# Modulation units as row products with a kept sum on VectorE, from a transposed weight

## The chip, the cores and the metric

One NeuronCore of a Trainium2 chip runs the whole program. The metric is the device time of one execution in microseconds. All tensors are float32; large products are split into a high and a low part in the rounded f32 format (fp32r), so that one product is three matmuls.

## What is computed

One inference step of a small diffusion backbone: two layers over 128 context tokens and 512 latent tokens of width 1024. Each layer is half a feed-forward block, a mixer of three head groups, and another half feed-forward block. Each of the three parts is modulated by vectors that come from a conditioning vector. Cut to what the change touches:

```python
def rmsnorm(x, g):
    y = x * lax.rsqrt(jnp.mean(x * x, axis=-1, keepdims=True) + EPS)
    return y * g

def layer(h, mod, p, lam_init, ctx):
    sh1, sc1, gt1, sh2, sc2, gt2, sh3, sc3, gt3 = jnp.split(mod[:, None, :], 9, axis=-1)
    u = rmsnorm(h, p["g_norm"][0]) * (1.0 + sc1) + sh1
    h = h + 0.5 * gt1 * swiglu(u, p["w_ff_in"][0], p["w_ff_out"][0])
    u = rmsnorm(h, p["g_norm"][1]) * (1.0 + sc2) + sh2
    y, cache = mix(u, p, lam_init, ctx)
    h = h + gt2 * y
    u = rmsnorm(h, p["g_norm"][2]) * (1.0 + sc3) + sh3
    h = h + 0.5 * gt3 * swiglu(u, p["w_ff_in"][1], p["w_ff_out"][1])
    return h, cache

for l in range(2):
    mod_ctx = silu(c_ctx)[None, :] @ w_ada[l] + b_ada[l]     # w_ada[l]: 1024 x 9216
    mod_lat = silu(c) @ w_ada[l] + b_ada[l]
    hp, cache_l = layer(hp, mod_ctx, p, lam_init, None)
    hs, _ = layer(hs, mod_lat, p, lam_init, ctx_l)
```

The two products with `w_ada` are what the change is about: two vectors of 1024 against a matrix of 1024 x 9216 in each layer, 75 MB of weights in all.

## The kernel before

**Layout.** The state h lies transposed in SBUF, features on partitions, tokens along the row (8 tiles of 128 x 640). All tokens, context and latent, go through one stream of products. The program runs, per layer: the first feed-forward half (FFN), the mixer (projection, three attentions, an order of work made by a planner of the kernel's own), the output projection (`wout`), and the second FFN half. A startup phase with an order written out by the planner stands ahead.

**An FFN half** (`ffn`) goes over 22 slices of the hidden width in four groups (6, 6, 5 and 5 slices). The first three slices are plain products in two token halves (`plain0`, `plain1`), the others a Strassen-like form of seven products per slice (`wino`). For each slice the weights are loaded (`load1`, 1 MB, two buffers shared with the other weight loads), and ScalarE and VectorE make the high and low parts. After the slices of a group come four steps `dd` of output products (`load2`, `unit2`), each followed by `update`, in which VectorE adds the gated PSUM result to h. The last group ends in `tail`, which starts the norm of the next part (`stats`, `norm`, `u_steps`): ScalarE squares, POOL and VectorE add them up, TensorE sums over partitions, and VectorE and ScalarE form the modulated input u.

**The modulations** come in 72 units of 256 columns of `w_ada` (`ada_units`), 36 per layer, in the order in which they are needed. The first 8 belong to startup. The other 64 are handed out by `pump`, which stands after slices (`pin`) and after output steps (`pout`); the table `ADA` says where and of which kind, one pair for each of the four FFN halves. A unit loads its 1024 x 256 block in two halves of 512 KB (`ada_raw`, tag `adaw`, two buffers, rows of 1 KB) on the SP queue. There are two kinds:

- "P" (`ada_unit_pe`, 21 of them): TensorE multiplies the blocks by the conditioning columns in strips of 32 columns (`ada_strip`, tile `adp`), ScalarE copies the result (`adrow`), and TensorE folds and turns it (tile `adt`).
- "D" (`ada_unit`, 43 of them): VectorE multiplies each of the eight 128 x 256 blocks by one conditioning value per partition and adds up, for both vectors (16 passes, `adacc`); TensorE transposes the two sums (4 transposes, `adt`), and VectorE reduces them along the row (`adred`).

`ada_finish` then adds the bias and forms the gates and scales (`mod`).

**What sets the order.** Each engine works its instructions in order. Outside the parts that the kernel's planner lays out, the order on each engine is made at build time by the framework, which goes by the order of the program and by when it expects an instruction to be ready: strips and VectorE passes of a unit are mixed into the surrounding slice work, and loads are put on the SP queue ahead of their use as buffers come free. PSUM has four small slots (`ps1`) and two large ones (`ps2`) for all of this; a slice's large slot is free once its SwiGLU steps (`post_steps`) have read it. `wpair`/`split` make the weight parts, `mm` (line 192) is the helper through which most matmuls go.

Of the kernel before, what the change touches and what calls it, by code (L numbers as in the profile page):

```python
# [32 lines left out]

_OUT = {(g, dd): "D" for g in (0, 6, 12, 17) for dd in range(2 if g == 17 else 3)}
ADA = (
    ({0: "P", **dict.fromkeys(range(2, 11), "P"), 14: "D", 16: "D", 19: "D"}, _OUT),
    ({0: "P", **dict.fromkeys((2, 3, 4), "P"), 8: "D", 14: "D", 19: "D"}, _OUT),
    ({**dict.fromkeys((4, 7, 10), "P"), 8: "D", 13: "D", 16: "D", 19: "D"}, _OUT),
    ({0: "P", **dict.fromkeys((2, 3, 4), "P")}, {}),
)  # L40
NP_ = 3
# [140 lines left out]
class Net:  # L182
# [139 lines left out]
    def ada_raw(self, l, s, u):  # L322

        c0 = s * D + u * 256
        for e in range(0, KD, QK):
            raw = self.adp.tile([P, QK, 256], F32, tag="adaw", name="adaw", bufs=2)
            self.nc.sync.dma_start(raw, self.a["w_ada"][l, e * P : (e + QK) * P, c0 : c0 + 256].rearrange("(k p) c -> p k c", p=P))
            for k in range(QK):
                yield e + k, raw[:, k, :]

# [4 lines left out]

    def ada_unit(self, l, s, u):
        nc, a = self.nc, self.a
        pt = self.ps1("adt")
        acc = [self.adp.tile([P, 256], F32, tag="adacc", name="adacc", bufs=2) for v in range(2)]
        for k, raw in self.ada_raw(l, s, u):  # L340
            for v in range(2):
                col = self.cs[:, 8 * v + k : 8 * v + k + 1]
                if k == 0:
                    nc.vector.tensor_scalar(acc[v], raw, col, None, ALU.mult)
                else:
                    nc.vector.scalar_tensor_tensor(acc[v], raw, col, acc[v], ALU.mult, ALU.add)  # L346
        for v in range(2):
            for j in range(2):
                nc.tensor.transpose(pt[:, (2 * v + j) * P : (2 * v + j + 1) * P], acc[v][:, j * P : (j + 1) * P], self.ident)
        red = self.sm.tile([P, 2, 2], F32, tag="adred", name="adred")  # L350
        nc.vector.tensor_reduce(red, pt.rearrange("p (v j c) -> p v j c", v=2, j=2), AX.X, ALU.add)
        self.ada_finish(l, s, u, red)

    def ada_unit_pe(self, l, s, u):

        ps = self.ps1("adp")
# [2148 lines left out]
```

## Time and profile before

| | us |
|---|---|
| median of 3 runs | 2755.49 (2755.48 to 2758.77) |
| profiled execution, its own time | 2755.85 |
| its span, first to last instruction | 2754.1 |
| TensorE matmul busy | 2671.8 |
| VectorE busy | 2147.6 |
| ScalarE busy | 1274.6 |
| mean granted TensorE clock | 0.987 |

The profile is one execution, with each instruction's start and duration. PE is TensorE's matmul row, DVE VectorE, ACT ScalarE, POOL GpSimd, SP the engine that issues the loads. Matmul durations overlap, since they are pipelined: the time that one takes up in the stream is the distance to the start of the next. A line number can be that of a helper; the names of the tiles (out<-in) tell what an instruction is for.

### The profile page before, as it was taken

Reading aid. Unit: us, or ns where it says so; the run is one execution under the profiler, and the core shown is the slowest. Engines: PE = TensorE matmul, PEld = TensorE weight load, DVE = VectorE, ACT = ScalarE, POOL = GpSimd, SP = SyncE. Lnnn points to the kernel's source line nnn. Section 1 sums busy time; section 2 is a strip of 40 time slices with the busy share of each in tenths; the row PEclk is TensorE's granted clock in tenths of the full one; section 3 lists DMA queues with packets and bytes.
Section 4 is the critical chain, followed back from the end, with each engine's and each line's share of the span. In section 5 each row is a group of like instructions: output and inputs, shape, how many; then the busy total and the mean of one; then the engine's idle time right before and its main releaser. Section 6 shows DMA issues by size and latency. Waiting matters only on the chain.

```text
span 2754.1 us, 46045 instructions
## 1 busy us (share of the span) xinstructions
PE 2671.8 (97%) x17549; PEld 2478.5 (90%) x17549; DVE 2147.6 (78%) x4580; ACT 1274.6 (46%) x2929; POOL 310.3 (11%) x506
## 2 busy tenths in 40 slices
PE   7999999999999999999999999999999999999998
PEld 5898999888778899999989999998887798999998
DVE  6687899776886678898987889987768847676765
ACT  5424334466675442433444334345657734343433
POOL 1000000142522100000010000003443220000000
PEclk8999999999999999999999999999999999999999
DMA  7454443322103324344333443433211033322232
GB/s 236 139 154 142 119 123 111 120 95 89 40 3 96 99 82 135 95 129 122 100 93 92 123 138 110 143 120 107 83 50 39 3 115 92 92 71 78 75 87 75
DMA packets 363348, 276.39 MB, mean 100 GB/s; under 512 B 25128, under 2 KB 350840, under 8 KB 363128
## 3 DMA queue, kind: packets, MB, share of 16 engines
q1 hardware_dynamic: 363128, 273.45, 33.2%
q8 instruction: 139, 2.28, 0.4%
q14 instruction: 81, 0.66, 0.1%
HBM read 259.25 MB, written 14.16 MB: 99 GB/s over the span
## 4 chain that ended last, share of the span: by engine, by line
PE 85%; DVE 7%; ACT 4%; POOL 1%; DMA 1%; issue 1%; SPq 0%; POOLq 0%; DVEq 0%; ACTq 0%
PE gu L192 35%; PE w L192 20%; PE zps L192 8%; PE ga L192 5%; PE wo L192 4%; PE tr L1294 3%; PE num L192 2%; PE sc L192 1%; PE y L1963 1%; PE z L192 1%; PE y L192 1%; PE adp L334 1%; DVE mx L1702 1%; DVE adacc L346 1%; DMA adaw<-in_w_ada 1%
## 5 line engine op out<-in xcount | busy, mean ns | idle before, releaser
L192 PE MATMUL gu<-u,wH 128*128 128x320 f32 x3504 | 625.8, 316 | 10.6 <-DVE pm L670 3.7
L192 PE MATMUL w<-hid,wH 128*128 128x384 f32 (+1 forms) x2816 | 621.1, 311 | 2.1 <-ACT wH L212 1.1
L192 PEld LDWEIGHTS gu<-u,wH 128*128 128x128 f32 x3504 | 542.3, 191 | 36.8 <-ACT X L1006 8.0
L192 PE MATMUL gu<-u,wL 128*128 128x320 f32 x3120 | 565.9, 314 | 1.6 <-DVE X L1008 0.6
L192 PEld LDWEIGHTS gu<-u,wL 128*128 128x128 f32 x3120 | 483.3, 189 | 19.9 <-ACT X L1006 6.6
L192 PEld LDWEIGHTS w<-hid,wH 128*128 128x128 f32 x2816 | 471.0, 188 | 7.5 <-ACT hid L694 3.6
L192 PE MATMUL w<-hid,wL 128*128 128x256 f32 (+1 forms) x1408 | 431.7, 310 | 0.9 <-DVE wL L213 0.8
L192 PEld LDWEIGHTS w<-hid,wL 128*128 128x128 f32 x1408 | 263.9, 188 | 2.5 <-DVE wL L213 2.3
L221 ACT CAST wH<-raw 128x512 fp32r<-128x512 f32 x266 | 163.6, 620 | 205.9 <-PE w L192 81.8
L346 DVE SCALAR_TENSOR_TENSOR adacc<-adaw,cs,adacc 128x256 f32<-128x256 f32 x602 | 255.5, 480 | 0.0
L739 POOL TENSOR_TENSOR ssum<-ssum,sq 128x384 f32<-128x384 f32 (+1 forms) x36 | 36.1, 1003 | 1886.3 <-ACT sq L738 1794.1
L192 PE MATMUL zps<-wH,u 128*128 128x512 f32 x704 | 242.0, 404 | 1.8 <-ACT u L888 1.7
L221 ACT CAST wL<-raw 128x512 fp32r<-128x512 f32 x266 | 163.9, 620 | 165.3 <-PE w L192 57.5
L931 DVE SCALAR_TENSOR_TENSOR h<-w,mod,h 128x128 f32<-128x128 f32 (+1 forms) x384 | 155.1, 436 | 105.4 <-PE w L192 104.3
L212 ACT CAST wH<-raw 128x640 fp32r<-128x640 f32 (+2 forms) x148 | 120.5, 816 | 223.7 <-PE w L192 161.9
L222 DVE TENSOR_TENSOR wH<-raw,wH 128x512 fp32r<-128x512 f32 x266 | 182.5, 688 | 42.8 <-ACT wH L221 40.9
L222 DVE TENSOR_TENSOR wL<-raw,wL 128x512 fp32r<-128x512 f32 x266 | 182.5, 688 | 38.0 <-ACT wL L221 36.7
L192 PEld LDWEIGHTS zps<-wH,u 128*128 128x128 f32 x704 | 131.8, 188 | 33.4 <-ACT u L888 5.3
L213 DVE TENSOR_TENSOR wL<-raw,wH 128x640 fp32r<-128x640 f32 (+2 forms) x148 | 137.7, 933 | 28.3 <-PE gu L192 14.6
L694 ACT CAST hid<-th 128x320 fp32r<-128x320 f32 x176 | 80.9, 459 | 148.7 <-DVE th L689 148.2
L192 PE MATMUL zps<-wL,u 128*128 128x512 f32 x352 | 138.0, 392 | 0.0
L1708 ACT ACTIVATE pr<-sc,mx 128x640 f32<-128x640 f32 (+1 forms) x160 | 113.5, 711 | 34.3 <-DVE mx L1702 33.2
(357 smaller groups left out, 4355.3 us busy)
## 6 DMA issues: line engine op xcount, KB each, us to landing
raw<-in_w_ff_in SPq DMA_DIRECT2D x176, 512.0 KB
adaw<-in_w_ada SPq DMA_DIRECT2D x144, 512.0 KB
raw<-in_w_ff_out SPq DMA_DIRECT2D x32, 768.0 KB
raw<-in_w_ff_out SPq DMA_DIRECT2D x32, 640.0 KB
rawi<-in_w_in SPq DMA_DIRECT2D x16, 1024.0 KB
rawo<-in_w_out SPq DMA_DIRECT2D x8, 1024.0 KB
bspill<-z SPq DMA_DIRECT2D x20, 256.0 KB
rawi<-in_w_in SPq DMA_DIRECT2D x8, 512.0 KB
```

The lines of the kernel that those rows point to most:

```text
L192: self.nc.tensor.matmul(out, lhsT, rhs, start=start, stop=stop, skip_group_check=go_on)
L212: nc.scalar.copy(H, raw)
L213: nc.vector.tensor_tensor(L, raw, H.bitcast(F32), ALU.subtract)
L221: nc.scalar.copy(w[:, 0], raw)
L222: nc.vector.tensor_tensor(w[:, 1], raw, w[:, 0].bitcast(F32), ALU.subtract)
L334: self.nc.tensor.matmul(ps[j : j + 32, 0:256], self.cs32[:, k, :], raw, start=k < 4, stop=k >= 4, tile_position=(0, j))
L346: nc.vector.scalar_tensor_tensor(acc[v], raw, col, acc[v], ALU.mult, ALU.add)
L694: nc.scalar.copy(self.hid[q][:, 0, c], st["th", hf])
L739: (nc.gpsimd if d in SSG else nc.vector).tensor_tensor(ssum[:, :w], ssum[:, :w], sq[:, :w], ALU.add)
L931: nc.vector.scalar_tensor_tensor(hh, ps[:, s0:s1], gm[:, v, d : d + 1], hh, ALU.mult, ALU.add)
L1294: nc.tensor.transpose(pt[:, i * P : (i + 1) * P], x, ident)
L1708: nc.scalar.activation(o, view(), AF.Exp, bias=bx["mx"], accum_out=bx["sums"])
```

## The change

All 64 units after startup are made in one way: `w_ada` is laid out transposed by the host, so that a block of 128 output columns is 128 rows of 1024. A unit loads two such blocks (512 KB each, 4 KB per partition), and for each block and each of the two vectors VectorE multiplies the rows by the conditioning vector, which is broadcast to all partitions, and keeps the sum along the row. Nothing of it goes through TensorE, PSUM or ScalarE. The broadcast vectors are made once after startup (`ada_rows`: two loads of 512 KB from one row each, two tanh passes of 1024 columns on ScalarE, two passes on VectorE). The first eight units stay on TensorE and read a copy of their columns in the old layout. The tables say how many units stand at a place: 20 in the first FFN half, 18 in the second and third, and two after each of the first two steps of both output projections (8); the units are used up before the fourth FFN half, whose entries find none left. The pump ahead of the second token half of slices 0 and 1 in `ffn` (`pin.get(0)`) is dropped. The DMA scratch in SBUF, which the framework reserves for descriptors that GpSimd writes, is set to 1 KB per partition.

```diff
-_OUT = {(g, dd): "D" for g in (0, 6, 12, 17) for dd in range(2 if g == 17 else 3)}
+_OUT = {(g, dd): n for g in (0, 6, 12, 17) for dd, n in enumerate((1, 1) if g == 17 else (2, 1, 1))}
 ADA = (
-    ({0: "P", **dict.fromkeys(range(2, 11), "P"), 14: "D", 16: "D", 19: "D"}, _OUT),
-    ({0: "P", **dict.fromkeys((2, 3, 4), "P"), 8: "D", 14: "D", 19: "D"}, _OUT),
-    ({**dict.fromkeys((4, 7, 10), "P"), 8: "D", 13: "D", 16: "D", 19: "D"}, _OUT),
-    ({0: "P", **dict.fromkeys((2, 3, 4), "P")}, {}),
+    (dict.fromkeys((3, 5, 8, 10, 14, 16), 1), _OUT),
+    (dict.fromkeys((4, 8, 14, 19), 1), _OUT),
+    (dict.fromkeys((4, 8, 14, 19), 1), _OUT),
+    (dict.fromkeys((3, 4), 1), {(0, 0): 2}),
 )
+ADO = 2, 2
...
+    def ada_rows(self):
+
+        nc = self.nc
+        self.csr = self.cp.tile([P, 2, D], F32, name="csr")
+        nc.sync.dma_start(self.csr[:, 0], self.a["c"][0].partition_broadcast(P))
+        nc.sync.dma_start(self.csr[:, 1], self.a["c_ctx"].partition_broadcast(P))
+        for v in range(2):
+            th = self.adp.tile([P, D], F32, tag="adaw", name="csth", bufs=2)
+            nc.scalar.activation(th, self.csr[:, v], AF.Tanh, scale=0.5)
+            nc.vector.scalar_tensor_tensor(self.csr[:, v], th, 1.0, self.csr[:, v], ALU.add, ALU.mult)
+
     def ada_unit(self, l, s, u):
-        nc, a = self.nc, self.a
-        pt = self.ps1("adt")
-        acc = [self.adp.tile([P, 256], F32, tag="adacc", name="adacc", bufs=2) for v in range(2)]
-        for k, raw in self.ada_raw(l, s, u):
+
+        nc = self.nc
+        red = self.sm.tile([P, 2, 2], F32, tag="adred", name="adred")
+        for j in range(2):
+            raw = self.adp.tile([P, D], F32, tag="adaw", name="adaw", bufs=2)
+            c0 = s * D + u * 256 + j * P
+            nc.sync.dma_start(raw, self.a["w_ada"][l, c0 : c0 + P])
             for v in range(2):
-                col = self.cs[:, 8 * v + k : 8 * v + k + 1]
-                if k == 0:
-                    nc.vector.tensor_scalar(acc[v], raw, col, None, ALU.mult)
-                else:
-                    nc.vector.scalar_tensor_tensor(acc[v], raw, col, acc[v], ALU.mult, ALU.add)
-        for v in range(2):
-            for j in range(2):
-                nc.tensor.transpose(pt[:, (2 * v + j) * P : (2 * v + j + 1) * P], acc[v][:, j * P : (j + 1) * P], self.ident)
-        red = self.sm.tile([P, 2, 2], F32, tag="adred", name="adred")
-        nc.vector.tensor_reduce(red, pt.rearrange("p (v j c) -> p v j c", v=2, j=2), AX.X, ALU.add)
+                out = self.adp.tile([P, D], F32, tag="adout", name="adout", bufs=1)
+                nc.vector.scalar_tensor_tensor(out, raw, 0.5, self.csr[:, v], ALU.mult, ALU.mult, accum_out=red[:, v, j : j + 1])
         self.ada_finish(l, s, u, red)
-
-    def ada_unit_pe(self, l, s, u):
...
     def startup(self, np_stack):
...
-                    nc.sync.dma_start(raws[i, e], a["w_ada"][l, e * 512 : (e + 1) * 512, c0 : c0 + 256].rearrange("(k p) c -> p k c", p=P))
+                    nc.sync.dma_start(raws[i, e], a["w_ada0"][e * 512 : (e + 1) * 512, c0 : c0 + 256].rearrange("(k p) c -> p k c", p=P))
...
         man.close()
+        self.ada_rows()
...
     def pump(self, kinds):
-        for e in kinds:
+        for e in range(kinds):
             x = next(self.adaq, None)
             if x is not None:
-                (self.ada_unit if e == "D" else self.ada_unit_pe)(*x)
+                self.ada_unit(*x)
...
     def ffn(self, l, j, gs):
...
-                self.pump(pin.get(0, ""))
...
     def wout(self, l):
...
                 for e in range(2):
                     for hf in range(2):
                         unit(2 * dd + e, hf)
+                self.pump(ADO[dd])
...
-    nc = _bacc.Bacc("TRN2", target_bir_lowering=False, num_devices=1)
+    nc = _bacc.Bacc("TRN2", target_bir_lowering=False, num_devices=1, dynamic_dma_scratch_size=1024)
...
+    host["w_ada0"] = np.ascontiguousarray(host["w_ada"][0, :, : 2 * D])
+    host["w_ada"] = np.ascontiguousarray(host["w_ada"].transpose(0, 2, 1))
```

## Rows read from the trace of the kernel before

**Rows 1.** The page's busy line: busy us (share of the span) and instructions by engine.
```profile
PE 2671.8 (97%) x17549; PEld 2478.5 (90%) x17549; DVE 2147.6 (78%) x4580; ACT 1274.6 (46%) x2929; POOL 310.3 (11%) x506
```
**Rows 2.** Stretches: three FFN halves, output projection; columns named in the first line.
```profile
core 0: us, PE busy (x) PEld busy (x) DVE busy (x) ACT busy (x) POOL busy (x), PEclk, DMA share, GB/s
75.00:515.00 440.00, 436.69 (x2951) 414.08 (x2949) 366.74 (x791) 166.05 (x323) 2.49 (x3) 1.00 0.44 131
960.00:1400.00 440.00, 438.78 (x2932) 427.27 (x2925) 382.15 (x814) 173.54 (x333) 6.28 (x6) 0.99 0.38 113
1450.00:1868.00 418.00, 415.18 (x2782) 403.53 (x2783) 366.48 (x790) 163.54 (x316) 3.31 (x4) 1.00 0.41 122
878.00:928.00 50.00, 50.00 (x337) 50.00 (x336) 20.93 (x40) 14.45 (x24) 11.15 (x8) 1.00 0.44 137
```
**Rows 3.** TensorE's timeline, one P unit: start us, us, engine, line, operation, tiles, count.
```profile
205.73 1.63 PE L192 MATMUL gu<-u,wL 128*128 128x320 f32 x10
207.29 1.05 PE L334 MATMUL adp<-adaw,cs 128*32 128x256 f32 x10
208.27 2.03 PE L192 MATMUL gu<-u,wH 128*128 128x320 f32 x12
210.23 0.63 PE L334 MATMUL adp<-adaw,cs 128*32 128x256 f32 x6
210.79 1.29 PE L192 MATMUL gu<-u,wL 128*128 128x320 f32 x7
211.92 0.50 PE L192 MATMUL adt<-fold,adrow 128*128 128x2 f32 x4
212.28 0.98 PE L192 MATMUL gu<-u,wL 128*128 128x320 f32 x5
```
**Rows 4.** TensorE's timeline, the transposes of one D unit.
```profile
162.82 0.28 PE L192 MATMUL w<-hid,wL 128*128 128x256 f32 x1
162.94 0.60 PE L349 MATMUL adt<-ident,adacc 128*128 128x128 f32 x4
163.30 0.59 PE L192 MATMUL w<-hid,wH 128*128 128x384 f32 x2
```
**Rows 5.** TensorE's timeline, start of the second FFN half of layer 0.
```profile
933.52 0.75 PE L192 MATMUL gu<-u,wH 128*128 128x320 f32 x4
...
938.13 0.62 PE L192 MATMUL gu<-u,wL 128*128 128x320 f32 x1
...
953.76 0.31 PE L192 MATMUL gu<-u,wL 128*128 128x320 f32 x1
...
960.72 0.90 PE L192 MATMUL gu<-u,wH 128*128 128x320 f32 x2
```
**Rows 6.** VectorE's timeline in the same stretch.
```profile
936.74 1.22 DVE L213 TENSOR_TENSOR wL<-raw,wH 128x1024 fp32r<-128x1024 f32 x1
...
959.30 0.48 DVE L689 TENSOR_TENSOR th<-th,gu 128x320 f32<-128x320 f32 x1
```
**Rows 7.** TensorE's timeline, start of layer 1's first FFN half; brackets: idle before, releaser.
```profile
1443.73 0.90 PE L192 MATMUL gu<-u,wH 128*128 128x320 f32 x2 [3.70 <-DVE pm L670]
```
**Rows 8.** Groups by line and shape: count | busy us, mean ns | idle before, releasers.
```profile
L1589 DVE TENSOR_TENSOR wL<-rawi,wH 128x1024 fp32r<-128x1024 f32 x32 | 39.4, 1246 | 9.7 <-ACT wH L1584 9.6
L689 DVE TENSOR_TENSOR th<-th,m 128x320 f32<-128x320 f32 x76 | 37.0, 487 | 0.7
L688 DVE SCALAR_TENSOR_TENSOR th<-th,m 128x320 f32<-128x320 f32 x76 | 37.0, 487 | 0.6 <-ACT th L684 0.6
L1708 ACT ACTIVATION_READ_ACCUMULATOR pr<-sc,mx 128x1 f32 x160 | 32.0, 200 | 0.0
L351 DVE TENSOR_REDUCE adred<-adt 128x4 f32<-128x512 f32 x43 | 29.4, 683 | 0.3 <-PE adt L349 0.2
L212 ACT CAST wH<-raw 128x1024 fp32r<-128x1024 f32 x20 | 20.6, 1044 | 10.4 <-PE gu L192 7.1 <-PE wo L192 3.2
```
**Rows 9.** A stretch, instructions that touch the unit loads: PE, PEld, DVE, clock, DMA.
```profile
75.00:515.00 440.00, 14.55 (x147) 4.64 (x144) 92.64 (x224) 1.00 0.44 131
```
**Rows 10.** The page's DMA queues: packets, MB, share of 16 engines.
```profile
q1 hardware_dynamic: 363128, 273.45, 33.2%
```

More of the change, by code (lines that the diff above doesn't have):

```diff
@@ L320, in ada_units @@
                         yield l, s, u
[L322 to L329, printed above, removed]
     def ada_strip(self, ps, k, raw):
@@ L354, in ada_unit_pe @@
-    def ada_unit_pe(self, l, s, u):
-        ps = self.ps1("adp")
-        for k, raw in self.ada_raw(l, s, u):
-            self.ada_strip(ps, k, raw)
-        row = self.adp.tile([P, 256], F32, tag="adacc", name="adrow", bufs=2)
-        self.nc.scalar.copy(row, ps[:, 0:256])
-        pt = self.ps1("adt")
-        for j in range(2):
-            self.mm(pt[:, 2 * j : 2 * j + 2], row[:, j * P : (j + 1) * P], self.fold, True, True)
-        self.ada_finish(l, s, u, pt[:, 0:4].rearrange("p (j v) -> p v j", v=2))
+    def ada_rows(self):
[7 more added lines that the diff above has]
+            nc.vector.scalar_tensor_tensor(self.csr[:, v], th, 1.0, self.csr[:, v], ALU.add, ALU.mult)
@@ L1083, in ffn @@
                     post(st, 1)
-                    self.pump(pin.get(f, ""))
+                    self.pump(pin.get(f, 0))
             prev = None
@@ L1092, in ffn @@
                     load2(0)
-                self.pump(pin.get(f, ""))
+                self.pump(pin.get(f, 0))
             rest(prev)
@@ L1102, in ffn @@
                             unit2(2 * dd + e, hf)
-                    self.pump(pout.get((g0, dd), ""))
+                    self.pump(pout.get((g0, dd), 0))
             if g0 == 0 and j == 0:
```

## The prediction

> **What bounds the kernel now.** I read the page's busy line first, then the stretches, then the order of TensorE's own instructions. TensorE is busy 2671.8 of 2754.1 us [rows 1]. In the three stretches that hold the slice loops of the first three FFN halves it is busy 436.69 of 440, 438.78 of 440 and 415.18 of 418 us, while VectorE has 366.74, 382.15 and 366.48 [rows 2]. So TensorE's instruction stream sets the time, and VectorE is second with 52 to 73 us of room per stretch, some 15%. A microsecond taken out of TensorE's stream comes off the end unless TensorE would have waited there anyhow; a microsecond put on VectorE is free only while that room lasts.
>
> **What is removed from TensorE.** 64 units come after startup, 21 of the "P" kind and 43 of the "D" kind. [Rows 3] shows one P unit inside the matmul stream. Single 320-column matmuls follow each other every 0.147 us and the last of a row ends 0.31 us after it began. So after the first row (205.73 + 1.63 - 0.31 + 0.147) the next was due at 207.20 and came at 208.27: 1.07 us for the first strips. By the same sum the others cost 0.65 us (due 210.14, came 210.79) and 0.36 us (due 211.92, came 212.28). One unit: 2.08 us. In a D unit only the four transposes lie on TensorE: the next product was due at 162.94 and came at 163.30, 0.36 us [rows 4].
>
> Not each of the 21 pays back. Fourteen lie in full streams like the one shown: 14 x 2.08 = 29.1 us. Six lie at the start of the two second FFN halves, three at each. There TensorE stops for 4.0 us (due about 934.1, next product 938.13) and for 6.8 us (due 953.9, next 960.72) [rows 5]. But the product at 938.13 reads a weight remainder that VectorE finished at 936.74 + 1.22 = 937.96, and the one at 960.72 needs a PSUM slot whose last reader ended at 959.30 + 0.48 = 959.78 [rows 6]; with a hand-over of about 0.2 us it could have begun near 960.0. So of 10.8 us only 0.7 come back at each, 1.4 for both, plus one fold of 0.36 each that falls later, 0.7. The last unit lies ahead of a place where TensorE waits 3.70 us for VectorE [rows 7]: arriving earlier only lengthens that wait, 0. The 43 transposes give 43 x 0.36 = 15.5. Sum: 29.1 + 1.4 + 0.7 + 15.5 = 46.7 us.
>
> **What VectorE gets.** A D unit now is 16 passes over 256 columns and a reduction. In the first stretch 224 such passes took 92.64 us, 0.414 each, and a reduction takes 0.683 [rows 8, 9]: 16 x 0.414 + 0.68 = 7.3 us, and 43 of them 314 us. The new unit is four products of 1024 columns with a kept sum, then the same finish. No row shows a product with a sum on VectorE. The nearest from below is the plain product of two f32 tensors of 1024 columns, 1.25 us [rows 8], about 1.15 back to back. From above I take the product followed by a pass of its own for the sum, two reductions of 512 columns: 1.25 + 1.37 = 2.6 us. A saving below the plain product is excluded, since both inputs still stream once. I take 1.3, near the lower end: the three-operand form is no dearer than the two-operand form here, 487 against 487 ns at 320 columns, and the separate sum read-out that ScalarE pays, 200 ns [rows 8], is an upper hint for the rest. So a unit is 5.2 us, 64 are 333 us against 314. Eight of them (42 us) go to the output projections, so the three FFN halves get 56 x 5.2 = 291, some 23 us less than now. In the first FFN half it is 20 x 5.2 = 104 against 102; in the second and third 94 each against 102 and 110. VectorE stays hidden there.
>
> One rule of the Trainium skill speaks against this. The page "Vector Engine (DVE) Microarchitecture Reference", section 7, Points that are easy to get wrong, says that the three-operand form with two sources in SBUF that aren't bf16 halves its throughput, because no port is left for the accumulator. By it a product would take about 2.3 us, an estimate from the plain product. The rows at 320 columns show no halving where no sum is kept; with a sum kept no row here shows it.
>
> **The rest.** *Startup:* two broadcasts of 512 KB, two ScalarE passes of 1024 columns (1.04 each) and two VectorE passes (1.25) [rows 8] are put ahead of the first FFN's own work, and the ScalarE casts and VectorE remainders of the third slice queue behind them. If all stood in line it would be 4.6 us; if all fits beside TensorE's remaining product of slice 1, nothing. I take 1. The broadcasts take the place of 1 MB of unit loads that went out first, and the slice loads behind them on the SP queue wait for 1 MB more at most. *Output projections:* four units each now run between the h updates. In the 50 us before the second FFN half VectorE is busy 20.93 [rows 2], so 29 us are free for 21. Queued behind them on VectorE are the h updates, the sums of squares and the norm; ScalarE's squares, POOL's sums and then TensorE's first products wait for those. Pieces of 1.3 us in front of such steps cost between 0 and 21 us per layer; I take 1.5 each, 3 in all, nearer to 0 by the free 29 us. *Unit loads:* as many of the same size on the same SP queue through two buffers, each released after two products (2.6 us) instead of eight passes (3.3); slice loads behind them wait less, 0. Doubled pumps ask for four loads in a row; VectorE may stand for a few us for the second pair, which the room of [rows 2] covers. *DMA scratch:* all kernel transfers are on the hardware queue [rows 10], none uses the scratch, 0; it makes room in SBUF only. The startup loads of layer 0 from a copy have the same rows of 1 KB, 0. ScalarE loses 21 small copies, off the path.
>
> Sum: -46.7 + 1 + 3 = -42.7. I add -2 for places where TensorE waits on a long D unit or its PSUM slot (the stretch 75 to 515 has 3.3 us idle [rows 2]; bounds 0 and 3.3). The profiled execution has 2755.85 us, 1.75 around its span of 2754.1, and the median of the runs is 2755.49, so the two stand for each other. 2755.85 - 44.7 = 2711 us.
>
> **The rivals.**
> *The output projections pay.* The four units fall ahead of the norm's last steps, and TensorE waits at the head of the second FFN halves for what VectorE does late. For it: VectorE is in order and its gaps there are short; against it: 29 us free for 21. Half of the bound in each layer, 10 us each instead of 1.5: 2711 + 17 = 2728. Chance 0.16.
> *More comes back.* With the strips gone VectorE and TensorE line up otherwise at the start of the second FFN halves and the two stops close. Against it: the two VectorE steps of [rows 6] have no strip before them. 2 x (4.0 + 6.1) = 20 more: 2691. Chance 0.08.
> *VectorE becomes the bound, and it is slower.* If keeping the sum makes a product cost twice the plain one, 2.3 us, a unit is 9.2. In the first FFN half VectorE's other work is 366.74 - 92.64 - 14 x 0.683 = 264.5 [rows 2, 8, 9]. TensorE's stream there would be 436.69 less 10 x 2.08 and 14 x 0.36, 410.8. So 146 us are left for 20 units, 7.3 each: it decides from a product of 1.8 us up. At 2.3 the stretch is 264.5 + 184 = 448.5, 8 over its 440; the second 280 + 166 = 446, 6 over; the third 257 + 166 = 423, 5 over; an output projection 20.9 + 36.8 = 57.7, 8 over its 50, twice. That is +35, less about 4 that the last FFN half keeps: 2787. At the upper bound of 2.6, 64 x 1.2 = 77 more, 2864. Against it: 487 against 487 ns. This is also what the skill's rule above would give. Chance 0.07.
> *No net change.* VectorE's pieces are three times as long as now and can't be put aside once begun. If each of the 256 holds up a step that TensorE needs by 0.17 us net, the gain is gone: 2755. Chance 0.04.
>
> **How the numbers follow.** The forecast has 0.65, with 2699 to 2724 (startup 0 to 4.6, projections 0 to 10 in all, waits 0 to 3.3). To hold 8 in 10 the range takes most of it, most of the first rival and a part of the second: 2694 to 2738. About 0.2%, 5.5 us, is what a measurement of this kernel can tell from no change. Faster by more: 0.65 + 0.16 + 0.08 = 0.89; within: 0.05, the last rival and a little of the slower one; slower: 0.06.
>
> **What would show it.** The groups of strips, folds and transposes after startup gone from TensorE, with some 45 us less busy time; the product with a sum on VectorE at 1.2 to 1.4 us, 256 of them, and VectorE's total within 25 us of now. The stops near 934 and 954 still there, released by the same two VectorE steps. Wrong would be: a product of 1.8 us or more, or VectorE above 95% in the slice loops; a TensorE wait at the head of the second FFN halves several us longer than today's; waits of TensorE for VectorE spread over the slice loops.

## The result

The changed kernel takes 2706.92 us (2703.81 to 2708.27), the kernel before 2755.48 beside it: a ratio of 0.9821, with an interval of 0.9809 to 0.9833. The forecast was 2711, with 2694 to 2738. The profiled execution has 2707.18 us around a span of 2705.2, 48.9 less than the span before.

The page's busy line and DMA queue, and the groups of the new instruction (count | busy us, mean ns | idle before, releaser), all of the kernel after:

```profile
PE 2608.1 (96%) x16957; PEld 2440.1 (90%) x16957; DVE 2165.1 (80%) x4363; ACT 1275.0 (47%) x2910; POOL 321.6 (12%) x506
```
```profile
q1 hardware_dynamic: 314264, 274.50, 33.2%
```
```profile
L348 DVE SCALAR_TENSOR_TENSOR adout<-adaw,csr 128x1024 f32<-128x1024 f32 x256 | 321.7, 1256 | 11.9 <-DMA adaw<-in_w_ada 11.0
L348 DVE DVE_READ_ACCUMULATOR adout<-adaw,csr 128x1 f32 x256 | 21.5, 84 | 0.0
```

Against [rows 1] and [rows 10], there are 48,864 packets fewer, and TensorE has 592 instructions and 63.7 us of (overlapping) busy time less, VectorE 17.5 us more. A product of 1024 columns with its sum takes 1256 ns, against 1246 for the plain one in [rows 8]; the sum has a row of its own, a read-out of 84 ns. VectorE's timeline shows that the read-out takes no turn of its own: it starts 1.15 us behind the product's start, just before the product's row ends, and the next instruction starts with it.

```profile
871.43 1.21 DVE L348 SCALAR_TENSOR_TENSOR adout<-adaw,csr 128x1024 f32<-128x1024 f32 x1
872.58 0.08 DVE L348 DVE_READ_ACCUMULATOR adout<-adaw,csr 128x1 f32 x1
872.58 0.34 DVE L917 SCALAR_TENSOR_TENSOR h<-wo,mod,h 128x128 f32<-128x128 f32 x1
```

So a product takes up 1.15 us of VectorE (871.43 to 872.58), and four of them 4.6.

**Where the time went.** Both kernels have the same 13,728 products of the FFN halves, projections and output projections on TensorE. The start of the same product in both traces gives the lead of the kernel after at that point:

| product | before, us | after, us | lead |
|---|---|---|---|
| first of layer 0's mixer projection | 528.34 | 498.22 | 30.1 |
| first of its output projection | 872.30 | 847.03 | 25.3 |
| first of the second FFN half | 933.08 | 911.78 | 21.3 |
| first output product of that half | 1026.59 | 996.34 | 30.3 |
| first of layer 1's mixer projection | 1875.24 | 1828.51 | 46.7 |
| first of its output projection | 2220.82 | 2174.47 | 46.4 |
| first of the last FFN half | 2281.62 | 2235.25 | 46.4 |
| first output product of that half | 2374.93 | 2325.55 | 49.4 |

The lead is not gained evenly: 4.8 us are lost again in layer 0's mixer (5.3 at its start, of which 0.6 come back later) and 4.0 in its output projection, and 9.0 are won at the start of the second FFN half of layer 0, three times what the same place brings in layer 1.

The loss at the mixer, TensorE's timeline (start us, us; brackets: idle before, releaser) of before and of after:

```profile
547.06 0.51 PE L192 MATMUL zps<-wH,u 128*128 128x512 f32 x1 [0.84 <-ACT u L888]
```
```profile
520.99 0.77 PE L192 MATMUL zps<-wH,u 128*128 128x512 f32 x1 [4.86 <-DVE u L866]
```

Up to this product both engines do the same instructions at the same distances. Then TensorE waits 4 us longer, for VectorE's last `u<-h,nbc` pass, whose result this product doesn't read. What they share is a PSUM slot: the norm's broadcast `nbc` takes the next of the four small slots in rotation, the planner's first `zps` takes slot 0. Each unit used to take one slot (D) or two (P), the new ones take none, so the rotation stands elsewhere: by the counter in the code `nbc` lies in slot 2 before the change, in slot 0 after it.

**Where the units ran.** Stretches of the kernel after; first all instructions, then those of the product's line alone (products and read-outs, two instructions each):

```profile
core 0: us, PE busy (x) PEld busy (x) DVE busy (x) ACT busy (x) POOL busy (x), PEclk, DMA share, GB/s
75.00:485.00 410.00, 406.52 (x2699) 397.45 (x2698) 363.93 (x708) 162.37 (x313) 3.15 (x3) 1.00 0.44 134
930.00:1370.00 440.00, 431.20 (x2854) 420.27 (x2852) 424.49 (x834) 181.25 (x344) 8.58 (x6) 1.00 0.46 142
1405.00:1820.00 415.00, 409.75 (x2704) 400.09 (x2704) 307.25 (x581) 164.24 (x317) 3.05 (x3) 0.99 0.33 97
```
```profile
75.00:485.00 410.00, 98.34 (x160) 1.00 0.44 134
930.00:1370.00 440.00, 135.43 (x220) 1.00 0.46 142
1405.00:1820.00 415.00, 29.47 (x48) 0.99 0.33 97
```

Eight rows make a unit: 20 units in the first stretch, 27.5 in the second and 6 in the third, where the tables put 20, 18 and 18. At layer 0's output projection six ran instead of four. The order that is built has put units of layer 1's first FFN half ahead into layer 0's second, where VectorE is now 96% busy, and left the third at 74%. Nothing in the prediction foresaw that; VectorE above 95% in a slice loop was one of its signs of being wrong, and it came although the time came out.

### The profile page after: what moved, and what is told of

It reads as the page before. It is cut to its first block, busy times and chain, and to the rows that moved or that the text cites. A ratio compares the mean times of both kernels' runs of the same rounds, so it can differ in the third digit from the quotient of the medians.

```text
span 2705.2 us, 44635 instructions
## 1 busy us (share of the span) xinstructions
PE 2608.1 (96%) x16957; PEld 2440.1 (90%) x16957; DVE 2165.1 (80%) x4363; ACT 1275.0 (47%) x2910; POOL 321.6 (12%) x506
## 4 chain that ended last, share of the span: by engine, by line
PE 78%; DVE 12%; ACT 4%; DMA 3%; issue 2%; POOL 1%; SPq 0%; DVEq 0%; POOLq 0%; ACTq 0%
PE gu L192 33%; PE w L192 18%; PE zps L192 8%; PE ga L192 5%; PE tr L1279 3%; PE wo L192 3%; DMA adaw<-in_w_ada 2%; DVE adout L348 2%; PE num L192 2%; PE sc L192 1%; PE y L1948 1%; PE z L192 1%; PE y L192 1%; DVE wL L213 1%; DVE mx L1687 1%
## 5 line engine op out<-in xcount | busy, mean ns | idle before, releaser
L192 PEld LDWEIGHTS gu<-u,wL 128*128 128x128 f32 x3120 | 481.9, 189 | 22.5 <-ACT X L992 7.0
L348 DVE SCALAR_TENSOR_TENSOR adout<-adaw,csr 128x1024 f32<-128x1024 f32 x256 | 321.7, 1256 | 11.9 <-DMA adaw<-in_w_ada 11.0
L725 POOL TENSOR_TENSOR ssum<-ssum,sq 128x384 f32<-128x384 f32 (+1 forms) x36 | 44.9, 1246 | 1839.3 <-ACT sq L724 1768.3
```

The source lines that it names most:

```text
L192: self.nc.tensor.matmul(out, lhsT, rhs, start=start, stop=stop, skip_group_check=go_on)
L348: nc.vector.scalar_tensor_tensor(out, raw, 0.5, self.csr[:, v], ALU.mult, ALU.mult, accum_out=red[:, v, j : j + 1])
L725: (nc.gpsimd if d in SSG else nc.vector).tensor_tensor(ssum[:, :w], ssum[:, :w], sq[:, :w], ALU.add)
```

## The experiments

**The PSUM slot (e1, and again as e11).** One line at the start of the mixer; run twice, each time beside the kernel before.

```diff
+        self.n1 = 1
         slot0 = self.nw + 1
```

> The changed kernel with one line more: the counter that hands out the four small PSUM slots is set to 1 at the start of each mixer, so that the norm's broadcast of the second token half lies in another slot than the first product of the planner's order. Theory (slot): in the changed kernel TensorE waits 5.04 us at 520.99 in layer 0 because that product needs the slot which VectorE reads to the end of the norm; without the shared slot the wait falls to about 1.0 us, as before the change (1.02) and as in layer 1 (1.03), and the half clock behind it (520.5 to 527.4) goes, worth another 0.8: 2702 us, ratio to the kernel before 0.9806. Rival (late chain): VectorE's norm itself is late at that place, so the wait stays about 5 us: 2707 us.

> The changed kernel with the PSUM slot alone once more, on the same chip as the run with the tied units, as its measure: 2700.5 us, within 2.

Measured: 2700.55 us, ratio 0.9795 (0.9781 to 0.981), and 2701.13, ratio 0.9804 (0.9789 to 0.9819). The first mixer product in the second of these traces:

```profile
515.95 0.49 PE L192 MATMUL zps<-wH,u 128*128 128x512 f32 x1 [0.84 <-ACT u L874]
```

The wait is the short one again: ahead of this product the run leads the kernel after by 1.0 us, at 530 us by 6.3, and from 572 us on by 5.4. The same 45 us of both, after first, then with the slot:

```profile
485.00:530.00 45.00, 38.41 (x195) 32.46 (x195) 34.85 (x94) 26.50 (x63) 11.14 (x21) 0.92 0.20 59
```
```profile
485.00:530.00 45.00, 42.41 (x220) 34.47 (x219) 35.39 (x98) 27.53 (x66) 12.02 (x23) 1.00 0.23 65
```

In the kernel after, the granted clock goes to half (1.2 GHz) late in the stop, from 519.9 to 526.8 us (the expectation has 520.5 to 527.4), and its mean is 0.92; without the stop it stays at 1.00. The slot was the cause of this wait. It is worth 5.3 us at the place, and 4.4 from 572 us on, of the some 6 us by which this version, the fastest found, lies below the changed kernel; 1.0 was there ahead of the mixer, and what makes up the rest is open.

**Products twice as dear (e2).**

```diff
-                nc.vector.scalar_tensor_tensor(out, raw, 0.5, self.csr[:, v], ALU.mult, ALU.mult, accum_out=red[:, v, j : j + 1])
+                for _ in range(2):
+                    nc.vector.scalar_tensor_tensor(out, raw, 0.5, self.csr[:, v], ALU.mult, ALU.mult, accum_out=red[:, v, j : j + 1])
```

> The changed kernel with every product made twice (the second overwrites the first), so that a product costs VectorE 2.3 us instead of 1.15: 256 more, some 295 us of VectorE. Theory (VectorE becomes the bound, as in the prediction's third rival): 2787 us, within 2770 to 2800, with VectorE above 95% in the slice loops of the first three FFN halves and TensorE waiting for it there. Rival (the room is larger than the sum by stretches says, because units can slip into the mixers): under 2730 us. Rival (each piece holds something up): linear in VectorE time, over 2800.

**A product of 1.75 us (e3).**

```diff
+                nc.vector.tensor_tensor(out[:, :512], raw[:, :512], self.csr[:, v, :512], ALU.mult)
                 nc.vector.scalar_tensor_tensor(out, raw, 0.5, self.csr[:, v], ALU.mult, ALU.mult, accum_out=red[:, v, j : j + 1])
```

> The changed kernel with a plain product of 512 columns (about 0.6 us) in front of every product with a sum, so that each costs VectorE about 1.75 us: some 155 us more of VectorE, just under the 1.8 us from which the prediction has VectorE decide. Theory (threshold): 2707 to 2715 us. Rival (no threshold, each VectorE microsecond costs TensorE the same share, 80 us for 295 as expected of the doubled product): 2748 us.

Measured: 2856.82 us (ratio 1.0365, 1.0349 to 1.038) and 2742.39 (0.9956, 0.9944 to 0.9967). Two stretches of the doubled product, then of the 1.75 us one:

```profile
75.00:515.00 440.00, 401.54 (x2540) 386.37 (x2539) 428.01 (x822) 154.91 (x300) 0.00 (x0) 0.96 0.36 112
960.00:1400.00 440.00, 404.59 (x2600) 392.83 (x2600) 423.16 (x825) 167.50 (x319) 7.75 (x5) 0.95 0.35 108
```
```profile
75.00:515.00 440.00, 424.74 (x2787) 412.30 (x2787) 418.60 (x810) 172.14 (x329) 6.92 (x6) 0.99 0.41 127
960.00:1400.00 440.00, 428.08 (x2858) 420.93 (x2857) 428.07 (x825) 179.37 (x340) 9.13 (x7) 0.99 0.39 120
```

With the doubled product VectorE sits at 96 to 97% and TensorE, 437 us of 440 before [rows 2], is down to 402 and 405. That VectorE becomes the bound is right; both sizes were wrong. The two times lie by the rivals, over 2800 and 2748, but a cost that is linear in VectorE's time, as these have it, isn't what the runs show: up to a product of 1.75 us, 155 us more of VectorE cost 35.5 us, 0.23 for each. From 1.75 to 2.3 us, 141 us more of VectorE cost 114 us, 0.81 for each. A part of that is TensorE's clock, which the first two rows have at 0.96 and 0.95. Drawn back from there, the line meets 2707 at a product of 1.75 - 35.5 / (0.81 x 256) = 1.58 us, not 1.8. That point is drawn from two runs, not measured.

**Products nearly free (e4).**

```diff
-                nc.vector.scalar_tensor_tensor(out, raw, 0.5, self.csr[:, v], ALU.mult, ALU.mult, accum_out=red[:, v, j : j + 1])
+                nc.vector.scalar_tensor_tensor(out[:, :64], raw[:, :64], 0.5, self.csr[:, v, :64], ALU.mult, ALU.mult, accum_out=red[:, v, j : j + 1])
```

> The changed kernel with every product cut to 64 of its 1024 columns (the sums, and with them the modulations, leave out the other 960): VectorE loses some 270 us of work, loads and order of units stay. Theory (VectorE is hidden but for a few places): the 4.0 us that layer 0's output projection lost and the waits of the slice loops, some 3 us, come back, the 5.04 us at the mixer's start stay: 2700 us, within 2697 to 2704. Rival (products fully hidden): 2707. Rival (pieces of 1.2 us still hold TensorE up all over): under 2695.

Measured: 2719.89 us (ratio 0.9865, 0.9848 to 0.9881), 13 us more than with whole products. All three readings missed. The product's group, then a place on VectorE and what followed on TensorE:

```profile
L348 DVE SCALAR_TENSOR_TENSOR adout<-adaw,csr 128x64 f32<-128x64 f32 x256 | 63.7, 249 | 62.5 <-DMA adaw<-in_w_ada 58.2
```
```profile
1044.35 0.22 DVE L348 SCALAR_TENSOR_TENSOR adout<-adaw,csr 128x64 f32<-128x64 f32 x1 [5.20 <-DMA adaw<-in_w_ada]
```
```profile
1057.88 0.63 PE L192 MATMUL gu<-u,wH 128*128 128x320 f32 x1 [4.66 <-DVE wH L222]
```

VectorE stands 58.2 us for unit loads, against 11.0 in the kernel after. The short products are put closer together and further ahead in the order (all of the second and third half's were done by 1200 us), the loads don't come so fast, and a waiting product at the head of VectorE's queue holds up the weight steps behind it. Around the place shown the run falls back by some 5.5 us against the kernel after. Another 2.5 us go at the head of layer 0's second FFN half, where the two stops of layer 1 are back (3.75 and 5.87 us; more on them under e6). So a shorter product alone brings nothing in this order; the loads need the spacing.

**Products without their sum (e5).**

```diff
+        nc.gpsimd.memset(red, 0.0)
...
-                nc.vector.scalar_tensor_tensor(out, raw, 0.5, self.csr[:, v], ALU.mult, ALU.mult, accum_out=red[:, v, j : j + 1])
+                nc.vector.scalar_tensor_tensor(out, raw, 0.5, self.csr[:, v], ALU.mult, ALU.mult)
```

> The changed kernel with the products kept but not their sums (the sums are set to zero, so the modulations are left out but for their bias). Theory (the sum is nearly free): the read-out of the sum, 84 ns by its own row, lies beside the next step, so the pitch of a product stays at about 1.15 us and the time at 2707 us, within 2703 to 2709. Rival (the sum is charged to the pass): a plain product is shorter than 1.22 us by 0.1 or more, VectorE's busy time falls by over 25 us beside the 21.5 of the read-outs, and the time by over 5.

Measured: 2713.58 us (ratio 0.9843, 0.9827 to 0.986), and the product's group is

```profile
L349 DVE SCALAR_TENSOR_TENSOR adout<-adaw,csr 128x1024 f32<-128x1024 f32 x256 | 318.6, 1244 | 12.8 <-DMA adaw<-in_w_ada 11.5
```

1244 ns without the sum, 1256 with it: the sum is free on VectorE, so that question is settled by the rows. The time, 7 us longer, is not in the expected range. Its trace places it: at the head of layer 1's first FFN half TensorE stops for 7.20 and 6.03 us (1380.33 and 1403.25), where the kernel after has one long stop, 3.9 at 1409.37, the one of [rows 7]. (Such stops are counted here from when the product was due, some 0.16 us more than in the brackets of a row.) At the head of layer 0's second FFN half, too, two stops are back, 3.93 and 5.87 us by their rows. With other operands in the units the order came out otherwise there. So 5 to 8 us hang on how the steps at the heads of the FFN halves fall, whatever the units cost; differences of this size between two built orders shouldn't be read as the price of the edit.

**No units in layer 0's output projection (e6).**

```diff
-    (dict.fromkeys((3, 5, 8, 10, 14, 16), 1), _OUT),
+    (dict.fromkeys((3, 4, 5, 8, 10, 13, 14, 16, 18, 19), 1), _OUT),
...
-                self.pump(ADO[dd])
+                self.pump(ADO[dd] if l else 0)
```

> The changed kernel without units in layer 0's output projection; the four stand in the first FFN half instead (after slices 4, 13, 18 and 19). Theory (the wait only moves): TensorE's 2.42 us at 900.21 and the 4.0 us that the output projection lost come back, but VectorE then reaches the head of the second FFN half no earlier, and the two stops there are those of layer 1, 3.91 and 6.03 us, instead of 0.71 and 2.29: from the first output projection product to the first output product of the FFN half 151 us as in layer 1 instead of 149.3, in all 2707 to 2711 us. Rival (the units cost what the projection lost): 2703 us.

Measured: 2711.13 us (ratio 0.9834, 0.982 to 0.9849), and at the head of the second FFN half

```profile
916.48 0.63 PE L192 MATMUL gu<-u,wL 128*128 128x320 f32 x1 [4.71 <-DVE wL L213]
938.21 0.87 PE L192 MATMUL gu<-u,wH 128*128 128x320 f32 x2 [5.87 <-DVE th L675]
```

The time and the two stops came as expected, but the run doesn't isolate what it meant to: 23 products still run between 850 and 950 us, since units of the second FFN half were put ahead into the projection (24 in the kernel after), and the wait of 2.4 us before the norm's sums is still there (900.28). What it shows is that the stops of layer 1 come back once those units are arranged otherwise. VectorE's timeline has the difference: ahead of the half's first product the kernel after (first two rows; product at 911.78) makes two of the slices' weight remainders, this run (third row; product at 910.58) one.

```profile
901.87 1.22 DVE L213 TENSOR_TENSOR wL<-raw,wH 128x1024 fp32r<-128x1024 f32 x1
906.41 1.22 DVE L213 TENSOR_TENSOR wL<-raw,wH 128x1024 fp32r<-128x1024 f32 x1
```
```profile
904.64 1.22 DVE L213 TENSOR_TENSOR wL<-raw,wH 128x1024 fp32r<-128x1024 f32 x1
```

The same holds at the second FFN halves of all the runs that have no strips there. With two remainders ahead (layer 0 of the kernel after and of both slot runs) the stops are 0.55 and 2.12 us by their rows; with one or none they are 3.75 or more and 5.4 or more. A late output projection is not what closes them: it takes 63.4 us in this run and 65.4 in layer 1 of e10, against 60.8 before, and the stops are whole. Which of the two orders is built was not set by an edit of its own.

**The DMA scratch alone (e7).**

```diff
-    nc = _bacc.Bacc("TRN2", target_bir_lowering=False, num_devices=1)
+    nc = _bacc.Bacc("TRN2", target_bir_lowering=False, num_devices=1, dynamic_dma_scratch_size=1024)
```

> The kernel before with the DMA scratch of 1 KB alone. Theory: nothing of it is used, 2755.5 us, within 2753 to 2759. Rival (the room in SBUF or the order that is built shifts): more than 5 us either way.

Measured: 2756.57 us beside 2756.58, ratio 1.0002 (0.9992 to 1.0011). No effect of its own.

**Only D units of the old kind, at the new places (e8).** The tables, `pump` and `wout` of the changed kernel in the kernel before, with its `ada_unit`.

```diff
-                (self.ada_unit if e == "D" else self.ada_unit_pe)(*x)
+                self.ada_unit(*x)
```

> The kernel before with all 64 units of the D kind (16 passes of 256 columns, four transposes and a reduction), at the places and in the numbers of the changed kernel, and the DMA scratch of 1 KB: the strips are gone from TensorE, but the row product is not there. Theory (the room on VectorE, not TensorE's strips alone, carries the gain): TensorE has 64 x 0.36 = 23 us more than in the changed kernel, and VectorE 64 x (7.3 - 4.9) = 154 us more, about what the added pass of 512 columns put on it (measured 35 us longer): 2707 + 23 + 35 = 2765, within 2750 to 2775, so no gain over the kernel before. Rival (taking the strips off TensorE is enough, VectorE's short passes fit in): 2730 us.

Measured: 2799.76 us, ratio 1.0156 (1.0141 to 1.0171), 43 us slower than before and 35 more than expected. TensorE's largest wait there (us in total, times, longest), which the kernel before doesn't have:

```profile
PE adt L350 <- DVE adacc L347: 24.5, 17, 2.9
```

Taking the strips off TensorE gains nothing where VectorE does the work in the old form. The four transposes of a D unit stand in TensorE's order at a fixed place, and when VectorE isn't done with the 16 passes, TensorE waits in front of them: the price isn't the 0.36 us of [rows 4] then but up to 2.9 more. These 24.5 us are the largest part seen of the 35 that were not expected.

**Row products for the D units alone (e9).** `ada_rows` and `ada_unit` of the changed kernel in the kernel before, beside its `ada_unit_pe` and with its own tables; the transposed weight is a second input.

```diff
...
+            nc.sync.dma_start(raw, self.a["w_adat"][l, c0 : c0 + P])
...
+    host["w_adat"] = np.ascontiguousarray(host["w_ada"].transpose(0, 2, 1))
```

> The kernel before with its 43 D units made as row products (from the transposed weight, with the broadcast vectors made after startup and the DMA scratch of 1 KB), and its 21 P units left as they are, all at their places of before. Theory (the strips are two thirds of the gain): only the transposes go, 43 x 0.36 = 15.5, less 1 for the startup and 2 for the D units' waits that also go: 2755.5 - 16.5 = 2739 us, within 2733 to 2744, so that the 21 P units account for the remaining 32 of the change's 49. Rival (the gain is the row product's, strips lie beside waits): 2720 us or less.

Measured: 2742.76 us beside 2757.29, ratio 0.995 (0.9934 to 0.9965): 14.5 us less, where 16.5 were expected. The number agrees, but the trace shows that it does so by luck. TensorE's largest wait there (us in total, times, longest) is the one for the shared PSUM slot, now in both layers:

```profile
PE zps L192 <- DVE u L887: 9.7, 2, 4.9
```

In the kernel before, this product waits 0.84 us in each layer. The 43 D units that no longer take a slot have moved the rotation here as well, and at the start of each mixer the lead of the profiled execution (17.6 us at its end) falls by 5.4 us. In the FFN halves it grows by some 25 us, where 43 x 0.36 = 15.5 were summed. So about 25 of the 56 us that the change brings with the slot mended come with the D units, and some 31 with the 21 P units and the new places; that is an estimate from these leads, since e9 with the slot mended was not run.

**Every unit tied to its place (e10).** Slot as in the first experiment, and

```diff
+        at = self.sm.tile([P, 1], F32, tag="adat", name="adat")
+        nc.vector.tensor_scalar(at, self.last, 0.0, 0.5, ALU.mult, ALU.add)
...
-                nc.vector.scalar_tensor_tensor(out, raw, 0.5, self.csr[:, v], ALU.mult, ALU.mult, accum_out=red[:, v, j : j + 1])
+                nc.vector.scalar_tensor_tensor(out, raw, at, self.csr[:, v], ALU.mult, ALU.mult, accum_out=red[:, v, j : j + 1])
...
             nc.vector.scalar_tensor_tensor(hh, ps[:, s0:s1], gm[:, v, d : d + 1], hh, ALU.mult, ALU.add)
+            self.last = hh[:, 0:1]
...
+                self.last = self.h[0][:, 0:1] if l == 0 else self.last
```

> The changed kernel with the PSUM slot of e1 and every unit tied to its place: the factor 0.5 comes from a one-column pass that reads the state h after its last update, so that no unit's products can be put ahead of the output steps before its place. In the order that is built the products then stand as 20, 20, 20, 12 in the four groups of the second and third FFN half, where the changed kernel has 33, 28, 27, 24 and then 26 and none after. Theory (room counts where the units really run): VectorE in the second FFN half's slice loops falls from 96% to under 90% and TensorE's waits there, some 8 us in 930 to 1370, halve: 3 to 5 us below the run with the slot alone, 2696 us. Rival (96% was room enough): the same as with the slot alone, 2700.5 within 2. Rival (the stops at the heads of the FFN halves follow the placement, not the load): up to 8 either way.

**Tied units between the slices only (e12).** The tables of e10 replaced, four units in each output projection as before.

```diff
+ADA = (
+    (dict.fromkeys(range(2, 22), 1), {}),
+    (dict.fromkeys(range(2, 20), 1), {}),
+    (dict.fromkeys(range(2, 20), 1), {}),
+    ({}, {}),
+)
```

> The run with tied units once more, but with no unit after an output step: one after each slice instead (20 slices of the first FFN half, 18 of the second and third), four in each output projection as before. Theory (it is the output steps): where the tied units stood between the updates of h, TensorE lost 5.3 us near 390, 3.2 near 1265 and 8 near 1728 beside the run with the slot alone, 16.5 in all; between the slices they cost nothing, so 2722 - 16.5 = 2705.5 us, within 2700 to 2709. Rival (being tied costs, wherever the place is, since a unit can't go where VectorE is idle): 2718 us or more.

Measured: 2722.06 us (ratio 0.9876, 0.986 to 0.9893) and 2764.02 (1.0028, 1.0019 to 1.0037), against 2701.13 with units free to move. Both theories fell, and the first run's rivals with them; the second run's rival, that being tied costs wherever the place is, came out. VectorE was spread evenly in the first, 377.02 of 440 us in the second FFN half instead of 422.37 with units free to move (both 935 to 1375 us), and it was 21 us slower. Between the slices, where tied units were to cost nothing, they cost 42 more. (The tie itself has a price: 64 passes of 0.148 us and 0.06 us per product for the other form, 25 us of VectorE; at the 0.23 that e3 paid for each of them this would be some 6 us, an estimate.) With units tied behind the output steps, VectorE and TensorE near 1728 us:

```profile
1728.24 1.28 DVE L350 SCALAR_TENSOR_TENSOR adout<-adaw,adat,csr 128x1024 f32<-128x1024 f32 x1
1729.44 0.09 DVE L350 DVE_READ_ACCUMULATOR adout<-adaw,adat,csr 128x1 f32 x1
1729.44 0.35 DVE L919 SCALAR_TENSOR_TENSOR h<-w,mod,h 128x128 f32<-128x128 f32 x1
```
```profile
1728.47 0.59 PE L192 MATMUL w<-hid,wH 128*128 128x384 f32 x2 [1.26 <-DVE h L919]
1731.40 0.77 PE L192 MATMUL w<-hid,wH 128*128 128x256 f32 x2 [2.34 <-DVE mod L360]
```

Products of 1.28 us stand between the h updates that TensorE waits for (the second of these waits ends with a unit's `mod` pass, which follows such an update). With units tied behind the slices, six slices and the output steps behind them:

```profile
1066.00:1143.00 77.00, 70.16 (x438) 66.96 (x437) 72.56 (x143) 35.56 (x74) 0.00 (x0) 0.96 0.39 120
1146.00:1195.00 49.00, 47.24 (x308) 46.75 (x307) 34.40 (x66) 10.72 (x17) 0.00 (x0) 0.97 0.43 133
```

VectorE is at 94% in the slices, which have grown to 77 us, and at 70% in the output steps. What each of the two kinds of stretch has free shows in the last FFN half of the kernel after, which has no units (rows: six slices, output steps, five slices, output steps).

```profile
2377.00:2443.00 66.00, 66.00 (x443) 64.60 (x442) 51.77 (x98) 34.50 (x70) 0.00 (x0) 1.00 0.31 87
2445.00:2491.00 46.00, 45.70 (x306) 45.15 (x306) 25.53 (x48) 10.31 (x17) 0.00 (x0) 1.00 0.28 81
2496.00:2549.00 53.00, 53.00 (x355) 51.72 (x354) 40.15 (x76) 26.76 (x54) 0.00 (x0) 1.00 0.30 85
2551.00:2591.00 40.00, 39.81 (x265) 38.81 (x264) 20.99 (x42) 7.80 (x14) 0.00 (x0) 1.00 0.30 86
```

The slices leave VectorE 14.2 of 66 and 12.9 of 53 us, the output steps 20.5 of 46 and 19 of 40. The same kinds of stretch in layer 0's second half of the kernel after, units free to move:

```profile
1047.00:1115.00 68.00, 67.39 (x446) 65.55 (x447) 66.51 (x127) 38.18 (x76) 0.00 (x0) 1.00 0.39 114
1117.00:1163.00 46.00, 46.00 (x313) 45.90 (x312) 45.10 (x94) 10.33 (x17) 0.00 (x0) 1.00 0.55 173
```

Both are at 98% on VectorE and TensorE loses 0.6 us of 114. A unit that can go anywhere fills 14 us in one kind of stretch and 20 in the other; six units tied into six slices want 6 x 4.6 = 28 us where 14.2 are free. That this, and not the tie's own 25 us, makes up most of the 21 and 63 us is read from these rows; a run that ties without a price wasn't made. Nor is it all: of the 23.4 us between the profiled executions of e11 and e10, 2.6 lie in layer 0's output projection and the head of the FFN half behind it, where e10 has the two stops whole, and 4.4 in layer 1's output projection.

## Why the prediction was right, and where it was not

*TensorE, -46.7.* The term of the strips holds, the term of the transposes was too small. In the first FFN half the lead grows from -0.97 us at 68 us to 22.5 at 265; ten P units, three D units and a wait of 1.1 us at 71.37 that falls away make 23.0. The eleven D units behind them bring 7.6 us instead of 4.0, and in e9 all 43 bring some 25 instead of 15.5. The sum priced the four transposes as if TensorE never waited next to them. In the kernel before, VectorE is full where such units stand,

```profile
398.00:412.00 14.00, 13.50 (x93) 12.93 (x93) 13.77 (x35) 2.12 (x4) 0.00 (x0) 1.00 0.64 182
```

and TensorE waits there behind the transposes for a weight remainder (0.30 us at 403.87, 0.29 at 414.65). That this is the whole of the difference is not shown. The -2 that was added for waits on D units is what stood for it.

The stops at the heads of the second FFN halves: in layer 1 they stand as foreseen without any strip,

```profile
2240.19 0.60 PE L192 MATMUL gu<-u,wL 128*128 128x320 f32 x1 [3.75 <-DVE wL L213]
2262.04 0.87 PE L192 MATMUL gu<-u,wH 128*128 128x320 f32 x2 [5.87 <-DVE th L675]
```

released by the two VectorE steps of [rows 6], and the lead there grows by 3.0 us: 0.7, one fold and one full unit, 3.1 by the sum. In layer 0 they did not stand: only 0.71 us at 916.31 and 2.29 at 939.39 are left, and that place gave 9.0 instead of 3.1.

```profile
916.31 0.56 PE L192 MATMUL gu<-u,wH 128*128 128x320 f32 x2 [0.55 <-ACT pm L643]
939.39 0.59 PE L192 MATMUL gu<-u,wH 128*128 128x320 f32 x2 [2.12 <-DVE th L675]
```

The forecast's second rival was right there by half: VectorE and TensorE do line up otherwise, since the order that is built has two weight remainders ahead of the half's first product (see e6). Whether it does is settled anew with each edit of the units; that it did so here was luck. From the first output projection product to the first output product of the FFN half it is 149.3 us in layer 0 and 151.1 in layer 1, both 3 to 5 below the 154 of before.

*Output projections, +3.* The total is near, 4.0 us lost in layer 0 and 0.0 in layer 1, but not as 1.5 in each. In layer 0, where six units ran instead of four, TensorE waits 2.42 us for the sums of squares, and its clock is at half from 902.2 to 905.6 us:

```profile
900.21 0.83 PE L192 MATMUL nst<-ones,ssum 128*128 128x1 f32 x6 [2.27 <-DVE ssum L725]
```

This is the first rival's sign, but its longer wait at the head of the FFN halves did not come.

*Startup, +1.* The kernel after is 0.97 us behind at 68 us, but not for the reason given: between 46 and 56 us it loses a lead of 2.5 us and falls behind, with the clock at half from 48.9 to 55.7, and the two ScalarE passes begin only at 65.8. The summed cost is seen in e11, which has the same startup and ran this stretch at full clock. There the added VectorE pass (first row) stands ahead of the step that TensorE waits for, 2.12 us instead of 1.09 in the kernel before: 1.0.

```profile
68.99 1.22 DVE L336 SCALAR_TENSOR_TENSOR csr<-csth,csr 128x1024 f32<-128x1024 f32 x1
```
```profile
70.66 0.55 PE L192 MATMUL gu<-u,wH 128*128 128x320 f32 x2 [2.12 <-DVE th L675]
```

From the start to the mixer the first FFN half gives 5.3 us more than 24.8, the sum for it (ten P, fourteen D, the startup); the D units and the wait at 71.37 above make up most of that.

*The missing term.* No line of the sum had the mixer, and it lost 4.8 us there. The step that failed is that units were costed as instructions and transfers, and not by the PSUM slots that they take. With the 9.0, the 5.3 and this, the sum's 44.7 and the measured 48.9 are close partly because misses cancel (5.9 and 5.3 us to one side, 4.8 to the other). That nearness is luck; the range, 17 us down and 27 up, is wide enough for each of them.

*The product, 1.3 us; a unit, 5.2; VectorE hidden.* The product takes up 1.15, a unit 4.6 and its finish; the lower end of the bounds was right, and the sum's read-out lies beside the next step. This also decides the rule of the Trainium skill that was named as a rival (page "Vector Engine (DVE) Microarchitecture Reference", section 7, Points that are easy to get wrong): the three-operand form with two f32 sources in SBUF does not run at half speed here, 1256 ns with a sum kept against 1246 for the two-operand form. Had it, the doubled product shows what would have come: 2857 us.

*The third rival's price, half of what it was.* At a product of 2.3 us the rival had 2787, 76 over the forecast; the chip took 2857, 150 over the changed kernel, and VectorE decides from about 1.6, not 1.8. The step that failed is the room: 410.8 - 264.5 us, 36% of the stretch, taken as one sum. The last FFN half leaves 76.5 of 258 us, 30%, split between slices and output steps. It didn't matter at 1.15 us; at 1.75 it was 35 us.

*Units at their places.* The sum put 20, 18 and 18 units where the tables have them. They ran elsewhere, and with units tied to those places the change brought 35 us instead of 56 (e10 and e11, both with the slot mended; the tie's own price is in it).

## What to carry to other kernels

A piece of work that no longer passes through the busiest engine is worth more than its instructions there: it also stops being tied to a place in that engine's order, and can fill whatever room the other engine has. Count that room by kind of stretch, not over a whole loop, and with the loads that the pieces wait for. When an edit changes how often a rotating buffer is taken, look at who gets which slot at the next phase; a product that waits for a pass whose result it doesn't read is the sign. And when a run's time agrees with its sum, compare the terms too: in e9 two misses of some 10 us cancelled.

## What was not expected of the hardware

- A sum kept by VectorE has an instruction row of its own, 84 ns (73 to 96), but costs the stream nothing: products are 1244 ns without it and 1256 with it, 1.15 us apart from the next step. On ScalarE the like row takes 200 ns [rows 8].
- In a stop of 5.0 us TensorE's granted clock fell to half (1.2 GHz), from 519.9 to 526.8 us; with the stop of 1.0 us at the same place it did not. The 4.0 us of wait were worth 5.3 us in the lead at 530 us, 4.4 from 572 us on.
